# Expert layer of a two-block network: 28 of 32 experts in 64-row blocks, both parts of the rows as 128 stationary columns, experts ordered by count, some low parts on GpSimd

## The chip, the cores and the metric

The kernel runs on one core of a Trainium2 chip. The metric is the device time of one execution in microseconds (us); lower is better. The time before is the median of three runs.

## What is computed

The reference is a network of two blocks on 512 tokens of 1024 features, in fp32. The first block has a hybrid mixer and then a mixture of 32 experts, and only this mixture is touched by the change. Each token chooses one of four groups and in it two of eight experts, so there are 1024 pairs of a token and an expert.

```python
def hierarchical_moe(h, w_rg, b_rg, w_re, b_re, w_e_gate, w_e_up, w_e_down):
    ...
    top_p, top_e = lax.top_k(jax.nn.softmax(le_sel, axis=-1), TOP_K)      # TOP_K = 2 of 8 in the group
    w_tok = p_g * top_p / jnp.sum(top_p, axis=-1, keepdims=True)
    ...
    def expert_rows(args):                                               # xb: rows of expert e
        xb, e = args
        return (jax.nn.silu(xb @ w_e_gate[e]) * (xb @ w_e_up[e])) @ w_e_down[e]
    ...
    contrib = ys[dest].astype(jnp.float32) * w_flat[order][:, None]
    return jax.ops.segment_sum(contrib, tok_sorted, num_segments=T).astype(h.dtype)
```

An expert has 1024 x 512 gate weights, as many up weights and 512 x 1024 down weights: 6 MiB in fp32 (6.29 MB), 201 MB for all. On the reference's inputs the router gives the experts, in order of their index, 26, 27, 11, 42, 12, 21, 30, 25, 12, 26, 30, 16, 13, 20, 39, 20, 67, 62, 44, 57, 26, 65, 40, 21, 31, 39, 29, 27, 27, 42, 46 and 31 tokens.

## The kernel before

Every dense product is made from fp32r parts. A chunk of 128 x 1024 weights is copied to a high part `whi` by ScalarE (L105, in `split`) and the rest is taken to a low part `wlo` by VectorE as raw less `whi` (L106). The other operand has two such parts too. A product is then three passes (`three`, L1672): high by high, high by low, low by high; low by low is left out.

The expert stage is `moe_experts` (L1725). It takes the experts by index. The order on the engines is the scheduler's, which follows the order of the program.

- `ex_rows` (L1650) makes the rows of three experts at once (GR = 3): a 0/1 matrix `s` of places (L1647, 128 x 336 per expert) selects the tokens, and for each of eight feature tiles eight matmuls of 252 columns (L1661) gather 84 rows (R = 84) of each of the three experts into PSUM tile `xg`. ScalarE writes the high part (L1665) and VectorE the low part (L1666). The eight steps run beside the experts of the group before, one at each `side` call.
- `ex_up` (L1680) takes four chunks of 1 MiB of gate and up weights, each in two halves, so eight weight tiles of 128 x 1024. For each, `three` issues 3 passes x 2 outputs = 6 matmuls of 512 columns (L1677, tile `gu`) with the 84 rows as stationary columns. At the end come the silu from PSUM (L1695) and the product with the up half (L1696).
- `ex_turn` (L1699) transposes the result to features on partitions (four transposes, L1704) and splits it (128 x 336).
- `ex_down` (L1709) takes two chunks of 1 MiB of down weights, so four weight tiles of six matmuls each (tile `py`), copies both halves of the result out of PSUM (L1721, ScalarE) and scatters the rows to DRAM by an indirect DMA issued from GpSimd (L1722).

So an expert has 12 weight tiles, 72 matmuls of 512 columns and six DMAs of 1 MiB, all issued in order by SyncE (L93). The down products of expert e - 1 follow the up products of expert e. Pool `raw` holds five chunks and pool `w` three pairs of parts, so that the split of a tile waits for the products of the tile three before it. VectorE, ScalarE and GpSimd work in their program order.

An expert with more than 84 tokens gets further blocks in a run-time loop, `moe_more` (L1760), after the stage. The router (`router`, L1536) ahead of the stage makes `qv`, the places by token and expert; `router_rest` (L1587) makes the tokens' weights, the rows' list `lst` for the scatter and the list of further blocks, after expert 1.

Of the kernel before, what the change touches and what calls it, by code (L numbers as in the profile page):

```python
# [9 lines left out]
F32 = mybir.dt.float32  # L10
# [9 lines left out]
T = 512  # L20
NT = 4
# [6 lines left out]
class Net:  # L28
# [32 lines left out]
    def setup(self, raw=5, w=3, res=10):  # L61
# [11 lines left out]
        # row h of a [40, T] tile of high parts, row 32 + h of low parts, summed onto every partition  # L73
# [48 lines left out]
    def dense_steps(self, p, w, x, first=True, last=True, off=0):  # L122
        """p += w^T x ; w = (hi, lo) with 128 columns per k tile, x = list of (hi, lo)."""
# [45 lines left out]
    def colsums(self, p, src, first=True, last=True, c0=0):  # L169
        """p[:, c0 + i] += sum over the partitions of src, tokens of tile i on partitions."""  # L170
# [4 lines left out]
    def sumsq(self, p, hs, gain=None, c0=0, first=True, last=True, direct=False):  # L175
        """Columns c0.. of p: the sum over all features of (h * gain)^2, tokens on partitions."""
# [15 lines left out]
    def bcast_cols(self, r):  # L192
        """[128 tokens, NT] columns -> [128, T] rows on every partition (PSUM)."""
# [68 lines left out]
    def narrow(self, src, n, x):  # L262
        """[128, NT * n] in PSUM: n columns of weights (src: n per k tile) on x."""
# [28 lines left out]
    def conv(self, z, taps, bias=None):  # L292
        """sum_j z[t - (n-1-j)] * taps[j] + bias ; taps: list of [128, 1]."""
# [14 lines left out]
    def ffn(self, hs, gain, w_up, taps, bias, w_down):  # L308
        """hs: 8 tiles [128, T]; w_up(i) / w_down(half, m) -> DRAM chunks. Returns the new residual tiles."""
# [44 lines left out]
# order of the first steps: decays, products, preparation and inversion of the first heads  # L354
# [3 lines left out]
def merge(*gens, fill=None):  # L358
    """Runs generators side by side, each spread evenly over the whole; fill = (generator, steps) ends with them."""
# [15 lines left out]
class Delta:  # L375
    def delta_consts(self):
        """Masks of the block inversion: for each block size the block left of the diagonal, and its transpose."""
# [15 lines left out]
        # same block, and place of the row in its block  # L393
# [8 lines left out]
    def rows(self, name, p, n):  # L402
        """Both parts of n rows in PSUM, for row_bcast."""
# [10 lines left out]
    def delta_first(self, w_gate16, w_head):  # L414
        """Weights of the step sizes and decays, and of q and k of head 0, the latter still in one part."""
# [76 lines left out]
    def dl_decays(self, p, r, dtB, alogB):  # L492
        """Step sizes beta and the decays' sums gc along each chunk, tokens on partitions."""
# [39 lines left out]
    def softplus(self, x, shape):  # L533
        """max(x, 0) + log1p(exp(-|x|)), the logarithm by its series in e / (2 + e)."""
# [57 lines left out]
    def dl_gates(self, w_head, ot, on):  # L592
        """The gates, and the heads' outputs times them."""
# [478 lines left out]
class Mixer:  # L1072
# [292 lines left out]
    def mixer(self, c):  # L1365
# [69 lines left out]
        for f in range(KD):  # L1435
# [8 lines left out]
            x1.append(t)  # L1444
            self.moe_feed(f, t)
        return x1, mod


NE = 32
R = 84  # L1450
GR = 3
BIG = 1024.0
FAR = 4096.0


class Moe:
# [579 lines left out]
```

## Time and profile before

| | us |
|---|---|
| time, median of 3 runs (range) | 2421.01 (2420.18 to 2422.82) |
| span of the profiled execution | 2423.5 |
| PE busy / VectorE / ScalarE / GpSimd | 2309.5 / 1751.2 / 1235.3 / 166.1 |
| expert stage, first to last silu of an expert | 469.2 to 1068.0 |
| moved by DMA | 374.31 MB |

The span of the profiled execution is its own time; it stands 2.5 us above the median of the three runs. Busy time of PE counts matmuls as they are pipelined: a matmul of 512 columns shows as 0.39 us, but one starts every 0.23 us. How long a row of operations takes is thus read from the starts, not from the sum of durations. The stretch from about 450 to 1075 us is the expert stage; the router lies just before it, the combination of the experts' rows just after it.

### The profile page before, as it was taken

The page shows a single profiled execution, that of the slowest core. Times are in us where ns is not written, and L with a number is a line of the kernel's source. Part 1 is how long each engine was busy: PE and PEld are TensorE (multiplying, and loading weights), DVE is VectorE, ACT ScalarE, POOL GpSimd, SP SyncE. Part 2 cuts the span into 40 slices and gives each one's busy share as a digit, 9 for nine tenths or more (in the row PEclk, how much of TensorE's full clock was granted, in tenths as well). Part 3 has the DMA queues.
Part 4 walks back from the last instruction along what each step waited for, and adds up shares of the span by engine and source line. Part 5 has one row for each costly group of instructions (what it writes and reads, how often), then busy time and mean ns, then how long its engine had stood idle before and what let it go on. Part 6 is the DMA issues. An engine that isn't in the chain of part 4 may idle for free.

```text
span 2423.5 us, 30698 instructions
## 1 busy us (share of the span) xinstructions
PE 2309.5 (95%) x11514; PEld 1832.1 (76%) x11514; DVE 1751.2 (72%) x2954; ACT 1235.3 (51%) x1966; POOL 166.1 (7%) x277
## 2 busy tenths in 40 slices
PE   3999999799999999989899999999999999999998
PEld 2788778576766677755788887888888888888886
DVE  7698874788888888876677767773775775763764
ACT  2253433577777777775444433442444664442441
POOL 4000100000000000000423310000000000000000
PEclk9999999899999999999999999999999999999998
DMA  7634142388888889874111111223212112223221
GB/s 283 234 120 141 36 156 106 137 302 321 330 322 329 325 332 338 336 278 175 53 53 36 53 53 70 88 71 129 98 61 94 70 53 105 82 72 134 83 76 43
DMA packets 64071, 374.31 MB, mean 154 GB/s; under 512 B 9648, under 2 KB 10032, under 8 KB 26032
## 3 DMA queue, kind: packets, MB, share of 16 engines
q1 hardware_dynamic: 60048, 367.97, 41.4%
q0 software_dynamic: 3584, 4.20, 0.5%
q8 instruction: 92, 1.51, 0.3%
q14 instruction: 59, 0.48, 0.1%
q10 hardware_dynamic: 288, 0.14, 0.0%
HBM read 365.85 MB, written 13.25 MB: 156 GB/s over the span
## 4 chain that ended last, share of the span: by engine, by line
PE 46%; DVE 4%; POOL 2%; ACT 2%; issue 1%; DMA 0%; SPq 0%; DVEq 0%; POOLq 0%; ACTq 0%
PE mm L135 13%; PE mm L132 13%; PE mm L129 13%; PE wk L1045 1%; PE wk L743 1%; POOL blk_x L712 1%; POOL blk_t L710 1%; PE wk L748 1%; ACT act L1012 0%; PE wk L993 0%; PE wk L1029 0%; PE po L780 0%; POOL act L714 0%; PE wk L752 0%; DVE act L303 0%
## 5 line engine op out<-in xcount | busy, mean ns | idle before, releaser
L105 ACT CAST whi<-raw 128x1024 fp32r<-128x1024 f32 (+2 forms) x653 | 664.9, 1025 | 725.3 <-PE mm L132 524.2
L106 DVE TENSOR_TENSOR wlo<-raw,whi 128x1024 fp32r<-128x1024 f32 (+2 forms) x652 | 768.7, 1190 | 216.9 <-ACT whi L105 205.5
L132 PE MATMUL mm<-act,whi 128*128 128x512 f32 x1968 | 777.6, 395 | 6.4 <-DVE act L106 4.2
L129 PE MATMUL mm<-act,whi 128*128 128x512 f32 x1968 | 778.6, 396 | 2.1 <-DVE res L472 1.2
L135 PE MATMUL mm<-act,wlo 128*128 128x512 f32 x1968 | 776.6, 395 | 0.3 <-DVE wlo L106 0.3
L132 PEld LDWEIGHTS mm<-act,whi 128*128 128x128 f32 x1968 | 371.6, 189 | 84.8 <-DVE act L106 5.7
L129 PEld LDWEIGHTS mm<-act,whi 128*128 128x128 f32 x1968 | 371.5, 189 | 78.2 <-ACT whi L105 2.7
L135 PEld LDWEIGHTS mm<-act,wlo 128*128 128x128 f32 x1968 | 371.4, 189 | 75.9 <-issue 2.6
L1677 PE MATMUL gu<-whi,act 128*84 128x512 f32 x1024 | 296.9, 395 | 0.4 <-DVE act L1666 0.4
L303 DVE SCALAR_TENSOR_TENSOR act<-act,vec,act 128x511 f32<-128x511 f32 (+2 forms) x272 | 205.9, 759 | 19.1 <-ACT act L298 12.5
L1677 PEld LDWEIGHTS gu<-whi,act 128*84 128x84 f32 x1024 | 151.0, 152 | 70.3 <-DVE act L1666 0.9
L1677 PE MATMUL gu<-wlo,act 128*84 128x512 f32 x512 | 160.2, 394 | 0.0
L1677 PE MATMUL py<-whi,act 128*84 128x512 f32 x512 | 144.2, 392 | 1.0 <-ACT act L105 1.0
L340 DVE TENSOR_TENSOR act<-mm,act 128x512 f32<-128x512 f32 x88 | 60.4, 689 | 84.3 <-PE mm L135 83.9
L1677 PEld LDWEIGHTS gu<-wlo,act 128*84 128x84 f32 x512 | 76.4, 151 | 42.9 <-DVE wlo L106 4.4
L1661 PEld LDWEIGHTS xg<-s,act 128*128 128x128 f32 x704 | 95.9, 192 | 13.5 <-issue 3.0
L1677 PEld LDWEIGHTS py<-whi,act 128*84 128x84 f32 x512 | 76.4, 151 | 37.8 <-ACT act L105 1.1
L105 ACT CAST act<-act 128x512 fp32r<-128x512 f32 x68 | 41.5, 620 | 116.3 <-DVE act L349 93.7
L1661 PE MATMUL xg<-s,act 128*128 128x252 f32 (+1 forms) x704 | 97.2, 282 | 2.9 <-DVE s L1647 2.9
L1181 DVE SCALAR_TENSOR_TENSOR act<-act,dw_half,act 128x482 f32<-128x482 f32 (+14 forms) x120 | 89.2, 744 | 0.5
L300 ACT ACTIVATE act<-act,vec 128x512 f32<-128x512 f32 x96 | 78.0, 814 | 12.2 <-DVE act L340 8.4
L1677 PE MATMUL py<-wlo,act 128*84 128x512 f32 x256 | 80.0, 394 | 1.7 <-DVE wlo L106 1.7
(484 smaller groups left out, 2256.4 us busy)
## 6 DMA issues: line engine op xcount, KB each, us to landing
raw<-in_w_gu_dram SPq DMA_DIRECT2D x128, 1024.0 KB, 5.2
raw<-in_w_dn_dram SPq DMA_DIRECT2D x64, 1024.0 KB, 5.4
raw<-in_f_up_dram SPq DMA_DIRECT2D x44, 1024.0 KB, 4.8
raw<-in_f_dn_dram SPq DMA_DIRECT2D x32, 704.0 KB, 4.0
ada<-in_w_ada_dram SPq DMA_DIRECT2D x32, 512.0 KB, 5.6
raw<-in_a_h_dram SPq DMA_DIRECT2D x16, 1024.0 KB, 5.0
raw<-in_w_ada_dram SPq DMA_DIRECT2D x8, 1024.0 KB, 9.0
raw<-in_w_glu_dram SPq DMA_DIRECT2D x4, 1024.0 KB, 7.4
```

Source lines behind the costliest of these rows:

```text
L105: self.nc.scalar.copy(out=hi, in_=src)
L106: self.nc.vector.tensor_tensor(out=lo, in0=src, in1=hi.bitcast(F32), op=ALU.subtract)
L129: mm(out=p, lhsT=wh[:, s], rhs=xh, start=first and k == 0, stop=False)
L132: mm(out=p, lhsT=wh[:, s], rhs=xl, start=False, stop=False)
L135: mm(out=p, lhsT=wl[:, s], rhs=xh, start=False, stop=last and k == n - 1)
L300: nc.scalar.activation(out=y, in_=z, func=ACTF.Identity, scale=taps[n - 1], bias=bias)
L303: nc.vector.scalar_tensor_tensor(out=y[:, s:], in0=z[:, :T - s], scalar=taps[j], in1=y[:, s:], op0=ALU.mult, op1=ALU.add)
L340: nc.vector.tensor_tensor(out=z, in0=p, in1=rb, op=ALU.mult)
L710: nc.gpsimd.tensor_tensor(out=x2[:, :, j + 1:], in0=R[:, :, j, j + 1:], in1=X[:, :, j:j + 1].to_broadcast([128, NT, B - 1 - j]), op=ALU.mult)
L1181: nc.vector.scalar_tensor_tensor(out=y[:, s:], in0=u[:, :T - s], scalar=taps[:, j, i:i + 1], in1=y[:, s:], op0=ALU.mult, op1=ALU.add)
L1661: nc.tensor.matmul(out=p[:, :n * R], lhsT=hT[k // 4][i][e][:, (k % 4) * 128:(k % 4) * 128 + 128], rhs=s[:, i, :n * R], start=i + e == 0, s ...
L1677: self.nc.tensor.matmul(out=o[:R], lhsT=x, rhs=y[:, i * T:(i + 1) * T], start=first and p == 0, stop=last and p == 2)
```

## The change

It replaces the 84-row blocks. Most hunks that only take out comments and docstrings are left out here.

- Experts are put into slots. Slots 0 and 1 are experts 0 and 1; the others follow by falling count (`moe_order`: a permutation from ranks, made with VectorE and small matmuls, while the rows of slots 0 and 1 are made from the unordered `q0`). SyncE reads the index of the expert of a slot from SBUF and addresses the weights by it.
- Slots 0 to 3 have blocks of 128 rows (RB) and the three passes as before. Slots 4 to 31 have blocks of 64 rows (RS). Their high and low parts lie side by side as 128 stationary columns, so there are two passes, with `whi` and with `wlo`, and low by low is no longer left out. The upper 64 partitions of the result belong to the low parts and are added to the lower 64: for gate and up by a product with `fold` (two unit matrices on top of each other) that turns at the same time, for the down product by a copy (ScalarE) and an addition (VectorE).
- Rows are made for groups of two (slots 0 to 3) or four slots, 256 columns a matmul; the steps are spread over the slots of the group before.
- In `ex_split` the low part of every fourth weight tile (2 and 6 of the up products, 2 of the down products) is made by GpSimd instead of VectorE.
- An expert with more rows than its slot has gets further blocks of 128 rows in `moe_more`.

```diff
+RB, RS = 128, 64
+NBIG, NFIX = 4, 2
+GROUPS = [[0, 1], [2, 3]] + [list(range(s, s + 4)) for s in range(NBIG, NE, 4)]
...
+    def moe_order(self, q, kr, **_):
+        nc = self.nc
+        t, t2, kc, rk = self.small([128, NE]), self.small([128, NE]), self.small([128, 1]), self.small([128, 1])
+        nc.vector.tensor_tensor(out=t, in0=kr, in1=self.mod32, op=ALU.mult)
+        nc.vector.tensor_reduce(out=kc, in_=t, axis=AX.X, op=ALU.add)
+        nc.vector.tensor_scalar(out=t2, in0=kr, scalar1=kc, scalar2=None, op0=ALU.is_gt)
+        nc.vector.tensor_reduce(out=rk, in_=t2, axis=AX.X, op=ALU.add)
+        self.perm = self.mconst("perm", [128, 128])
+        nc.vector.tensor_scalar(out=self.perm, in0=self.agree, scalar1=rk, scalar2=None, op0=ALU.is_equal)
...
     def ex_rows(self, hT, qs, xs, r):
...
-            nc.scalar.activation(out=hi, in_=p[:, :n * R], func=ACTF.Identity, bias=b)
+            nc.scalar.activation(out=x4[:, :, 0], in_=p3, func=ACTF.Identity, bias=b)
+            nc.vector.scalar_tensor_tensor(out=x4[:, :, 1], in0=p3, scalar=b, in1=x4[:, :, 0].bitcast(F32), op0=ALU.add,
+                                           op1=ALU.subtract)
...
+    def ex_products(self, outs, l, w, first, last):
+        wh, wl = w
+        n = l.shape[-1]
+        ps = ((l, wh), (l, wl)) if n == 2 * RS else ((l[:, :RB], wh), (l[:, :RB], wl), (l[:, RB:], wh))
+        for p, (x, y) in enumerate(ps):
+            for i, o in enumerate(outs):
+                self.nc.tensor.matmul(out=o, lhsT=x, rhs=y[:, i * T:(i + 1) * T], start=first and p == 0,
+                                      stop=last and p == len(ps) - 1)
+
+    def ex_split(self, src, c):
+        hi, lo = self.fixed[1] if self.fixed else self.w_pair()
+        self.nc.scalar.copy(out=hi, in_=src)
+        e = self.nc.gpsimd if c % 4 == 2 and not self.fixed else self.nc.vector
+        e.tensor_tensor(out=lo, in0=src, in1=hi.bitcast(F32), op=ALU.subtract)
+        return hi, lo
...
+    def ex_act(self, pg, pu, r):
+        nc = self.nc
         s, a = self.act(), self.act()
+        if r == RB:
+            nc.scalar.activation(out=s, in_=pg, func=ACTF.Silu)
+            nc.vector.tensor_tensor(out=a, in0=s, in1=pu, op=ALU.mult)
+            return a, None
+        nc.scalar.copy(out=s, in_=pg)
+        nc.vector.tensor_copy(out=a, in_=pu)
+        return s, a
+
+    def ex_turn(self, a, u):
...
+        for j, t in enumerate((a, u)):
+            for k in range(4):
+                nc.tensor.matmul(out=p[:, j * 256 + k * RS:j * 256 + (k + 1) * RS], lhsT=t[:, k * 128:k * 128 + 128],
+                                 rhs=self.fold, start=True, stop=True)
+        s, h = self.act(), self.act(F32R)
+        g, m = s[:, :256], s[:, 256:]
+        nc.scalar.activation(out=g, in_=p[:, :256], func=ACTF.Silu)
+        nc.vector.tensor_tensor(out=m, in0=g, in1=p[:, 256:], op=ALU.mult)
+        h4 = h.rearrange("p (k e c) -> p k e c", k=4, e=2)
+        self.split(h4[:, :, 0], h4[:, :, 1], m.rearrange("p (k c) -> p k c", k=4))
...
     def ex_down(self, a, w_dn, rows):
...
-            nc.scalar.copy(out=y[:R, i * T:(i + 1) * T], in_=ys[i][:R])
...
+            t = self.tl("y", "y", [128, D])
+            nc.scalar.copy(out=t[:RS], in_=ys[RS:])
+            nc.vector.tensor_tensor(out=y[:RS], in0=ys[:RS], in1=t[:RS], op=ALU.add)
+        nc.gpsimd.indirect_dma_start(out=self.yd, out_offset=bass.IndirectOffsetOnAxis(ap=rows[:r], axis=0), in_=y[:r],
...
+        def expert(e):
+            if e < NFIX:
+                return e
+            if e not in ids:
+                ids[e] = nc.values_load(self.order[0:1, e:e + 1], engines=(mybir.EngineType.SP,), min_val=0, max_val=NE - 1,
+                                        skip_runtime_bounds_check_because="a permutation of the 32 experts, by ranks of distinct keys")
+            return ids[e]
```

## Rows read from the trace of the kernel before

**Rows 1.** The page: busy us, share and instructions of each engine.

```profile
PE 2309.5 (95%) x11514; PEld 1832.1 (76%) x11514; DVE 1751.2 (72%) x2954; ACT 1235.3 (51%) x1966; POOL 166.1 (7%) x277
```

**Rows 2.** Busy time by stretch: span, engines, granted clock, DMA share, GB/s.

```profile
550.00:650.00 100.00, 99.51 (x491) 69.29 (x490) 86.85 (x92) 78.40 (x95) 4.64 (x5) 1.00 0.89 331
1100.00:1110.00 10.00, 9.04 (x36) 3.60 (x35) 6.79 (x10) 7.59 (x14) 1.59 (x2) 1.00 1.01 428
```

**Rows 3.** Waits from 550 to 1030 us: total us, times, longest.

```profile
ACT whi L105 <- PE gu L1677: 73.6, 138, 0.9
```

**Rows 4.** The silu at each expert's end: duration ns, first and last start.

```profile
L1695 ACT ACTIVATE act<-gu x32: 577/584/598, 469.2 to 1068.0; 84x512 f32<-84x512 f32 x32
```

**Rows 5.** Timeline: start, us, engine, line; runs of equal operations merged.

```profile
1034.94 1.07 PE L1677 MATMUL py<-whi,act 128*84 128x512 f32 x4
455.07 1.10 PE L1661 MATMUL xg<-s,act 128*128 128x252 f32 x8
1187.31 1.00 PE L743 MATMUL wk<-act,act 128*128 128x64 f32 x8
787.20 3.48 DVE L106 TENSOR_TENSOR wlo<-raw,whi 128x1024 fp32r<-128x1024 f32 x3
790.40 3.07 ACT L105 CAST whi<-raw 128x1024 fp32r<-128x1024 f32 x3
```

**Rows 6.** Groups from 200 to 1150 us, by shape: busy us, mean ns of one.

```profile
L1677 PE MATMUL gu<-whi,act 128*84 128x512 f32 x1024 | 296.9, 395 | 0.4 <-DVE act L1666 0.4
L135 PE MATMUL mm<-act,wlo 128*128 128x512 f32 x304 | 121.3, 399 | 0.0
L106 DVE TENSOR_TENSOR wlo<-raw,whi 128x1024 fp32r<-128x1024 f32 x422 | 508.8, 1223 | 106.9 <-ACT whi L105 99.5
L1666 DVE SCALAR_TENSOR_TENSOR act<-xg,mod,act 128x252 fp32r<-128x252 f32 x80 | 37.8, 475 | 3.2 <-ACT act L1665 3.2
L1721 ACT COPY y<-py 84x512 f32<-84x512 f32 x64 | 34.2, 585 | 7.5 <-PE py L1677 4.8
L1722 POOL DMA_INDIRECT yd<-y,lst x32 | 30.4, 949 | 565.7 <-ACT y L1721 559.6 <-DVEq L1767 6.1
L1696 DVE TENSOR_TENSOR act<-act,gu 84x512 f32<-84x512 f32 x32 | 21.6, 674 | 0.2 <-ACT act L1695 0.2
L106 DVE TENSOR_TENSOR act<-xg,act 128x336 fp32r<-128x336 f32 x32 | 16.0, 500 | 0.3 <-ACT act L105 0.3
L1647 DVE TENSOR_TENSOR s<-slot,act 128x336 fp32r<-128x336 f32 x32 | 15.0, 502 | 0.0
```

**Rows 7.** Timeline: GpSimd's elementwise work beside VectorE's.

```profile
1098.42 2.06 DVE L1829 SCALAR_TENSOR_TENSOR res<-wk,mod,res 128x512 f32<-128x512 f32 x3
1099.04 1.28 POOL L1818 TENSOR_TENSOR act<-act,act 128x512 f32<-128x512 f32 x1 [12.47 <-ACT act L1817]
...
1232.19 0.62 POOL L699 TENSOR_TENSOR act<-blk_e,place 128x256 f32<-128x256 f32 x1 [6.97 <-DVE blk_e L696]
1232.22 1.14 DVE L303 SCALAR_TENSOR_TENSOR act<-act,vec,act 128x511 f32<-128x511 f32 x1
1278.65 1.28 POOL L714 TENSOR_TENSOR act<-blk_x,blk 128x512 f32<-128x512 f32 x1
1278.73 1.74 DVE L303 SCALAR_TENSOR_TENSOR act<-act,vec,act 128x511 f32<-128x511 f32 x1
1350.89 1.22 DVE L106 TENSOR_TENSOR wlo<-raw,whi 128x1024 fp32r<-128x1024 f32 x1
1351.05 2.17 POOL L714 TENSOR_TENSOR act<-blk_x,blk 128x512 f32<-128x512 f32 x1
```

**Rows 8.** The group of L303 on the page: busy us, mean ns.

```profile
L303 DVE SCALAR_TENSOR_TENSOR act<-act,vec,act 128x511 f32<-128x511 f32 (+2 forms) x272 | 205.9, 759 | 19.1 <-ACT act L298 12.5
```

**Rows 9.** Busy time by stretch around gaps of PE; the columns of rows 2.

```profile
332.00:339.00 7.00, 5.34 (x13) 4.23 (x14) 6.28 (x8) 1.67 (x2) 0.00 (x0) 0.51 0.18 65
...
1350.00:1356.00 6.00, 4.70 (x36) 4.18 (x35) 3.91 (x14) 2.44 (x13) 3.65 (x6) 1.00 0.46 160
```

More of the change, by code (lines that the diff above doesn't have):

```diff
@@ L1463, in moe_prep @@
             nc.gpsimd.iota(c[name], pattern=pattern, base=base, channel_multiplier=ch, allow_small_or_imprecise_dtypes=True)
-        self.rev, self.slot, self.tokv = c["rev"], c["slot"], c["tokv"]
+        self.rev, self.slot, self.tokv, self.bonus, self.step = (c[n] for n in ("rev", "slot", "tokv", "bonus", "step"))
+        for e in range(NFIX):
+            nc.vector.tensor_scalar(out=self.bonus[:, e:e + 1], in0=self.bonus[:, e:e + 1], scalar1=float(FIRST * (NFIX - e)),
+                                    scalar2=None, op0=ALU.add)
@@ L1660, in ex_rows @@
                 for e in range(2):
[L1661 to L1662 removed]
+                    nc.tensor.matmul(out=p[:, :n * r], lhsT=hT[k // 4][i][e][:, (k % 4) * 128:(k % 4) * 128 + 128],
+                                     rhs=s[:, i, :n * r], start=i + e == 0, stop=i + e == NT)
             x = self.act(F32R)
[L1664 removed]
@@ L1709, in ex_down @@
     def ex_down(self, a, w_dn, rows):
         nc = self.nc
-        ah, al = a
-        ys = [self.tl("ps", "py", [128, T], F32, bufs=2) for _ in range(2)]
+        r = RS if not isinstance(a[0], tuple) else RB
+        ys = self.tl("ps", "py", [128, D], F32, bufs=1)
+        outs = [ys[:, i * T:(i + 1) * T] for i in range(2)]
         for q in range(2):
@@ L1725, in moe_experts @@
-    def moe_experts(self, hT, w_gu, w_dn, rest):
-        group = lambda e: [self.qv[:, i, 0:4] for i in range(e, min(e + GR, NE))]
-        x, xn = None, [[] for _ in range(GR)]
-        first = self.ex_rows(hT, group(0), xn)
+                wp = self.ex_split(w[:, j * 1024:(j + 1) * 1024], k)
+                if r == RS:
+                    self.ex_products(outs, a[k], wp, k == 0, k == 3)
+                else:
+                    self.three(outs, a[k], wp, k == 0, k == 3)
+        y = self.tl("y", "y", [128, D])
@@ new lines, in ex_down, with three @@
+        if r == RB:
+            nc.scalar.copy(out=y, in_=ys)
+        else:
+            t = self.tl("y", "y", [128, D])
+            nc.scalar.copy(out=t[:RS], in_=ys[RS:])
+            nc.vector.tensor_tensor(out=y[:RS], in0=ys[:RS], in1=t[:RS], op=ALU.add)
+        nc.gpsimd.indirect_dma_start(out=self.yd, out_offset=bass.IndirectOffsetOnAxis(ap=rows[:r], axis=0), in_=y[:r],
+                                     in_offset=None, bounds_check=2 * T - 1, oob_is_err=False)
+    def three(self, outs, l, w, first, last):
+        (lh, ll), (wh, wl) = l, w
+        for p, (x, y) in enumerate(((lh, wh), (lh, wl), (ll, wh))):
+            for i, o in enumerate(outs):
+                self.nc.tensor.matmul(out=o, lhsT=x, rhs=y[:, i * T:(i + 1) * T], start=first and p == 0,
+                                      stop=last and p == 2)
@@ L1730, in moe_experts, with weights @@
+    def moe_experts(self, hT, w_gu, w_dn, order, rest):
+        nc = self.nc
+        xn = [[] for _ in GROUPS[0]]
+        first = self.ex_rows(hT, [self.q0[:, :, e] for e in GROUPS[0]], xn, RB)
         next(first)
+        order()
+        ids, rows = {}, None
         a = t = None
-        def side(q):
-            nonlocal t
-            if e:
-                next(rows, None)
+        def expert(e):
[5 more added lines that the diff above has]
+            return ids[e]
+        def weights(w, e, m):
+            i = expert(e)
+            return w[i, m] if e < NFIX else w[bass.ds(i, 1), m].rearrange("a p c -> (a p) c")
+        def side(q):
+            nonlocal t, due
+            if e and rows:
+                due += 8 / sides
+                while due > 0.5:
+                    next(rows, None)
+                    due -= 1
@@ L1743, in before @@
                 next(first, None)
+        starts = {g[0]: i for i, g in enumerate(GROUPS)}
+        due = 0
         for e in range(NE + 1):
-            if e % GR == 0:
-                x, xn = xn, [[] for _ in range(GR)]
-                if e + GR < NE:
-                    rows = self.ex_rows(hT, group(e + GR), xn)
+            if e in starts:
+                for _ in rows or ():
+                    pass
+                i = starts[e]
+                x, xn = xn, []
+                rows = None
+                if i + 1 < len(GROUPS):
+                    g = GROUPS[i + 1]
+                    xn = [[] for _ in g]
+                    rows = self.ex_rows(hT, [self.qv[:, s, 0:4] for s in g], xn, 256 // len(g))
+                sides, due = 4 * (len(GROUPS[i]) - (e == 0)), 0
             if e < NE:
-                b = self.ex_up(x[e % GR], lambda m: w_gu[e, m], side, before)
+                b = self.ex_up(x[e - GROUPS[i][0]], lambda m: weights(w_gu, e, m), side, before)
                 if e == 1:
```

196 lines of the change are left out of this document (120 added, 76 removed).

## The prediction, made before the change was run

> **What bounds the kernel now.** The page first: PE is busy for 95% of the span, VectorE for 72%, ScalarE for 51%, GpSimd for 7% [rows 1]. Such shares are means over stages, so the second view is the stretch that the change touches. From 550 to 650 us PE has 99.5 of 100 us, VectorE 87, ScalarE 78, GpSimd 5, and the DMA engines are at 0.89 with 331 GB/s [rows 2]. Third, who waits: ScalarE's split of weights waits for PE's products, 138 times in 480 us [rows 3]. So in the expert stage PE is the bound, and VectorE and the transfers are not far behind. Last, its pace: from the first silu to the last there are 31 experts in 598.8 us, 19.3 us each [rows 4].
>
> PE's own work explains that pace. Four matmuls of 512 columns show 1.07 us, of which the last 0.39 is its own length, so one starts every 0.23 us; eight gathers of 252 columns start every 0.117 us [rows 5]. 72 x 0.23 = 16.6 us, and 88 gather steps x 8 x 0.117 over 32 experts = 2.6 us; with the four transposes 19.4. There is nothing in the 19.3 us but PE.
>
> **What the change takes from PE.** An expert with 64 rows has two passes, 48 x 0.23 = 11.0 us. The gathers of four experts are 8 steps x 8 matmuls of 256 columns, 64 x 0.118 / 4 = 1.9 us. The turn is eight fp32 products of 64 columns; eight such show 1.00 us, one every 0.11 us [rows 5], so 0.9. PE needs 13.8 us instead of 19.4. 128 stationary columns instead of 84 cost nothing that the rows show: a matmul of 512 columns lasts 399 ns with 128 and 395 ns with 84 [rows 6].
>
> Were PE the only limit, 28 experts would save 28 x 5.5 = 154 us. So the question is what is late next.
>
> **The transfers.** An expert's 6.29 MB stay. Just after the stage the DMA engines moved 428 GB/s over 10 us [rows 2], at which 6.29 MB take 14.7 us. That is a floor below the next one. SyncE reads an index per slot before it issues; it has one issue every 3.2 us (19.3 / 6), and I put this at nothing, up to 1 us an expert if the read is slow.
>
> **ScalarE.** Three copies of 128 x 1024 show 3.07 us, one every 1.0 us [rows 5]: 12.1 us, and about 2.7 us for gathers, the copies out of PSUM, silu and split (by columns from the 0.585 us of a 512-column copy [rows 6]). 14.8 us: not the next bound either.
>
> **VectorE.** Three low parts show 3.48 us, so one starts every 1.13 us although it lasts 1.22 [rows 5, 6]; I take 0.09 off each operation for that. Nine low parts stay here: 10.2. Low parts of the rows: two of 0.39, in 24 of 28 experts, 0.7. Places: 256 columns by the 336 of now, 0.3. Copy of the up half from PSUM, by the 0.674 of the product that it replaces: 0.6. Product and split of the turn on 256 columns: 0.3 each. Addition of the two halves of the result on 1024 columns, as long as a low part: 1.1. Together 13.5 us [rows 6]. With all 12 low parts it would be 16.9.
>
> **GpSimd.** An elementwise operation with two inputs took 1.28 us for 512 columns and 0.62 for 256 [rows 7]; in a line 1024 take 2.6 us, three 7.8 us, and the scatter 0.95 [rows 6]. It has 18 us for that. But these operations are not free for VectorE. The low part takes `raw` and `whi`, both in SBUF, and rows 7 show what happens when such an operation meets GpSimd: L303, 0.76 us as a rule [rows 8], took 1.74 when it began 0.08 us after a 1.28 us operation of GpSimd, and 1.14 after one of 0.62. The other way round, GpSimd's L714 took 2.17 us when it came during a low part, and ended 1.1 us after it. They run one after the other. VectorE loses 0.38 us to 256 columns and 0.98 to 512; in a line that is 2.2 for 1024 (upper end 2.6, the whole operation). I take 2.25: 6.7 us an expert.
>
> The Trainium skill has this as a rule (SBUF — State Buffer, section Who interferes with whom): an operation of VectorE with two SBUF inputs and one of GpSimd that reads SBUF exclude each other, and the later one waits for the whole instruction. The trace agrees on the exclusion but shows 0.98 of 1.28 us lost. By the page's rule three whole operations of 2.6 us, an estimate, would be 1.1 us more an expert, and the change about 31 us later than by my sum.
>
> VectorE and GpSimd together then have 13.5 + 6.7 = 20.2 us, more than now, unless VectorE does something else while GpSimd works. It can: the three L1829 from 1098.42 on, which take one input from PSUM, took 2.06 us together, less than three times L303's 0.76, though L1818 ran for 1.28 us beside them [rows 7]. Of the 13.5 us such operations are: low parts of the rows 0.7, copy 0.6, product 0.3, addition 1.1, in all 2.7. How many fall beside GpSimd is the uncertain term, between 0 and 2.7.
>
> I lay the operations out by hand, with the ring of three pairs. A split waits for the low part of the tile three before it, so VectorE is one or two tiles ahead of PE. What needs PE's end of tile 3, 7 or the last down tile becomes ready when VectorE has done two tiles more, just where GpSimd's tile (2, 6, 2 of the down) comes next. The addition lands beside up tile 2, the first rows' low part beside up tile 6, the copy beside down tile 2: 1.1 + 0.4 + 0.6 = 2.1 us. The product, the second rows' low part and the split come while low parts are queued. That gives 20.2 - 2.1 = 18.1, and I allow 0.4 (0 to 0.8) for VectorE waiting for others: 18.5 us an expert.
>
> GpSimd's queue: the scatter of an expert stands behind the addition, and a low part that stands behind the scatter would wait for both. By hand the addition ends before GpSimd's tile 2 does, so I put nothing here; the other order makes the addition uncovered.
>
> **Sum.** The last 28 experts: from the fourth silu on the pace now is 19.3 (the mean of [rows 4]); 28 x (18.5 - 19.3) = -22. The first four keep three passes: PE 16.6 us plus gathers; they have 16 gather steps where the stage now has 12, +4, and VectorE with GpSimd at about 20 us is as late as PE, +4 (0 to 8). `moe_order` adds some ten operations of 0.2 to 0.3 us on VectorE while the first gathers run, +1 (0 to 3); the evacuation after the last expert, copy then addition instead of two copies, +1. Constants at the start, +1. In all -22 + 11 = -11: the profiled execution would go from 2423.5 to 2412, and the median, 2.5 us below its span now, to 2410.
>
> **The rivals.** (a) Slower: the uncovered sum. If the scheduler puts the addition and the copy behind a low part, 0.4 us at most lies beside GpSimd: 20.2 - 0.4 + 0.4 = 20.2, 28 x 0.9 + 11 = +36, 2457. It decides where less than 1.7 us of the 2.7 is covered (28 x 0.4 us = the 11 us of the rest). For it: VectorE keeps a fixed order, and the program order has these operations behind low parts. Against: my layout. 0.33.
>
> (b) The exclusion costs little, because VectorE anyway waits at those times, and the stage falls to what ScalarE and the transfers allow, 15.5 us: -106 + 11, 2326. Against: all of rows 7 show exclusion. 0.10.
>
> (c) Near break-even, 18.8 to 19.1 us: 2418 to 2426, 0.15.
>
> (d) PE, which now waits, gets the low clock. The granted clock fell to 0.51 of 2.4 GHz, that is 1.2 GHz, in 7 us where PE had gaps of about 2 us, and stayed at 1.00 with PE busy for 78% of 6 us [rows 9]. A wait for GpSimd's tile is some 1.3 us (its 2.6 us less the products of one or two tiles, 0.9 us each, that PE still has). If it fell, 13.8 us would be up to 27.6 and the stage over 100 us longer. 0.03.
>
> (e) It doesn't do what it says: further blocks. In order of count, slots 2 and 3 get the experts with 67 and 65 tokens, and the next has 62, under 64. So no pass of `moe_more`, unless the chip counts otherwise; a pass would cost at least the 14.7 us of its transfers. 0.01.
>
> **How the numbers follow.** The forecast, 18.1 to 18.8 us an expert (2398 to 2418), has 0.38. A difference of 0.2%, 5 us, is about what a measurement of this kernel can tell from no change. Faster: 0.38 + 0.10 = 0.48. Same: 0.15. Slower: 0.33 + 0.03 + 0.01 = 0.37. As both signs are likely, the forecast's own range is 2398 to 2418. The wide one leaves out (b) below and the worst of (a), (d) and (e) above: all 2.7 us covered, no waits and none of the additions, 28 x (17.5 - 19.3) = -50, gives 2371; nothing covered with 0.2 us of waits, 20.4, gives 2463, and the upper price of the exclusion a little more: 2367 to 2468.
>
> **What would show it.** Two passes: 32 matmuls of `gu` and 16 of `py` for each of slots 4 to 31, and PE no longer busy all the time in the stage. The exclusion: low parts on VectorE of up to 3.5 us, and GpSimd's of 2.6 us or more, one beginning where the other ends. The layout: the addition, the copy and a rows' low part beside GpSimd's operations. A pace between silus of neighbours near 18.5 us. I am wrong if VectorE and GpSimd run side by side at their own speed, if PE is still busy all the time, or if VectorE is idle for more than 1 us an expert.

## The result, and the profile after

The changed kernel takes 2537.09 us (median of 4 runs) where the kernel before takes 2420.60: a ratio of 1.048, 95% interval 1.046 to 1.049. It is slower, and above the range of the prediction. The profiled execution has a span of 2535.3 us, 111.8 more than before.

The page's engine row of the changed kernel answers [rows 1]: PE has 12 us less, VectorE 63 us more although 96 low parts have left it, GpSimd 262 more.

```profile
PE 2297.5 (91%) x11062; PEld 1840.3 (73%) x11062; DVE 1814.4 (72%) x2919; ACT 1225.9 (48%) x1949; POOL 428.6 (17%) x379
```

Busy time by stretch, the view of [rows 2], for 100 us in the middle of the stage:

```profile
850.00:950.00 100.00, 82.50 (x359) 60.75 (x358) 80.89 (x70) 64.72 (x80) 38.56 (x18) 0.90 0.79 284
```

PE is no longer the bound, and neither is any other engine: VectorE has 81 of 100 us, ScalarE 65, the transfers 284 GB/s instead of 331. When nothing is full, the time is in waits. The granted clock is 0.90, too.

The pace, the view of [rows 4]: the silu of the first four experts (L1795), and the copy of the gate half out of PSUM that ends the up products of the other 28 (L1798); duration in ns, first and last start:

```profile
L1795 ACT ACTIVATE act<-gu x4: 589/590/600, 472.2 to 541.5; 128x512 f32<-128x512 f32 x4
...
L1798 ACT COPY act<-gu x28: 576/587/589, 562.1 to 1171.9; 128x512 f32<-128x512 f32 x28
```

From the fourth silu to the last copy, 28 experts take 1171.9 - 541.5 = 630.4 us, **22.51 us each** instead of 19.27: +91. The first four take 69.3 instead of 59.1 (+10), they begin 3 us later, and from the last copy to the last scatter it is 20.4 instead of 13.9 us (+7): together 111 of the 112.

The low parts, the view of [rows 6] (562 to 1050 us; duration is the number after the comma), and below them the same line over the whole run with its shortest, median and longest duration in ns:

```profile
L1774 DVE TENSOR_TENSOR wlo<-raw,whi 128x1024 fp32r<-128x1024 f32 x194 | 323.7, 1692 | 52.7 <-ACT whi L1772 52.6
L1774 POOL TENSOR_TENSOR wlo<-raw,whi 128x1024 fp32r<-128x1024 f32 x65 | 166.1, 2555 | 192.3 <-PE py L1766 94.7 <-ACT whi L1772 86.1 <-PE gu L1766 7.8
```

```profile
L1774 DVE TENSOR_TENSOR wlo<-raw,whi x288: 1204/1216/3762, 416.6 to 1184.4; 128x1024 fp32r<-128x1024 f32 x144
...
L1774 POOL TENSOR_TENSOR wlo<-raw,whi x96: 2352/2372/3887, 431.3 to 1184.4; 128x1024 fp32r<-128x1024 f32 x96
```

Most of VectorE's low parts (205 of 288) take 1.2 us as before, the others up to 3.76. One expert's timeline shows how (start, us; in brackets the idle time and what ended it; weight loads and some lines left out):

```profile
853.47 0.69 DVE L1799 COPY act<-gu 128x512 f32<-128x512 f32 x1 [0.82 <-PE gu L1766]
...
857.36 2.37 POOL L1774 TENSOR_TENSOR wlo<-raw,whi 128x1024 fp32r<-128x1024 f32 x1 [5.79 <-PE py L1766]
...
858.21 2.60 DVE L1774 TENSOR_TENSOR wlo<-raw,whi 128x1024 fp32r<-128x1024 f32 x1 [1.07 <-ACT whi L1772]
...
859.78 0.73 PE L1766 MATMUL py<-wlo,act 128*128 128x512 f32 x2 [1.43 <-POOL wlo L1774]
...
862.89 1.22 DVE L1844 TENSOR_TENSOR y<-py,y 64x1024 f32<-64x1024 f32 x1 [0.60 <-ACT y L1843]
...
864.38 1.63 POOL L1845 DMA_INDIRECT yd<-y,lst  x1 [4.65 <-ACT act L1751]
865.16 0.47 DVE L1752 SCALAR_TENSOR_TENSOR act<-xg,mod,act 128x256 fp32r<-128x256 f32 x1
...
866.04 2.36 POOL L1774 TENSOR_TENSOR wlo<-raw,whi 128x1024 fp32r<-128x1024 f32 x1
866.22 5.54 DVE L1774 TENSOR_TENSOR wlo<-raw,whi 128x1024 fp32r<-128x1024 f32 x3 [0.59 <-ACT whi L1772]
...
868.45 0.74 PE L1766 MATMUL gu<-wlo,act 128*128 128x512 f32 x2 [1.97 <-POOL wlo L1774]
```

VectorE's low part from 858.21 ends at 860.81, 1.08 us after GpSimd's ended (859.73): it ran behind it. Three from 866.22 take 5.54 instead of 3.48. And the copy (853.47), the addition (862.89) and the rows' low part (865.16), which the prediction had put beside GpSimd's low parts, stand where GpSimd has none: it waits for PE, for the addition, or issues the scatter. (The bracket of the scatter names L1751, which ended last before it, at 864.31; by the program the scatter reads what the addition writes, and that ended at 864.11.)

The low parts are not the only work that is held up. The places (L1730) have two SBUF inputs too, which the prediction did not price; the same line in the changed kernel and in e1, the kernel without GpSimd's low parts, 562 to 1050 us:

```profile
L1730 DVE TENSOR_TENSOR s<-slot,act 128x256 fp32r<-128x256 f32 x16 | 17.2, 1092 | 3.8 <-PE xg L1745 3.8
```

```profile
L1730 DVE TENSOR_TENSOR s<-slot,act 128x256 fp32r<-128x256 f32 x16 | 6.1, 419 | 0.2
```

To compare kernels, VectorE's time per expert is taken apart, from the starts and durations of all its instructions between the fourth and the last end of an expert's up products: busy; lost (of the busy time, what low parts take over 1.215 us each; the places come on top, 0.46 us an expert in the changed kernel); idle. Beside it the pace and the time:

| kernel | GpSimd's tiles | pace | busy | lost | idle | time |
|---|---|---|---|---|---|---|
| before | none | 19.27 | 16.60 | 0.10 | 2.67 | 2421 |
| after | up 2, 6, down 2 | 22.51 | 18.49 | 4.35 | 4.02 | 2537 |
| e1 | none | 18.65 | 17.04 | 0.01 | 1.61 | 2419 |
| e2 | as after, 8 columns read | 19.16 | 13.83 | 0.04 | 5.33 | 2435 |
| e5 | as after, 4 pairs | 23.70 | 19.36 | 5.28 | 4.34 | 2571 |
| e6 | as after, PE kept busy | 22.37 | 18.86 | 5.03 | 3.51 | 2535 |
| e8 | up 6 | 20.17 | 17.88 | 1.90 | 2.29 | 2464 |
| e11 | up 0, 4, down 0 | 19.79 | 15.96 | 1.87 | 3.83 | 2462 |
| e12 | up 0, down 0 | 18.79 | 15.46 | 0.44 | 3.33 | 2432 |
| e9 | none, copy on ScalarE | 17.89 | 16.34 | 0 | 1.55 | 2401 |
| e13 | as e12, copy on ScalarE | 18.99 | 15.94 | 1.52 | 3.05 | 2439 |

### The profile page after: what moved, and what is told of

It is laid out like the page before. It is cut to its first block, busy times and chain, and to the rows that moved or that the text cites. A ratio compares the mean times of both kernels' runs of the same rounds, so it can differ in the third digit from the quotient of the medians.

```text
span 2535.3 us, 30370 instructions
## 1 busy us (share of the span) xinstructions
PE 2297.5 (91%) x11062; PEld 1840.3 (73%) x11062; DVE 1814.4 (72%) x2919; ACT 1225.9 (48%) x1949; POOL 428.6 (17%) x379
## 4 chain that ended last, share of the span: by engine, by line
PE 44%; DVE 4%; POOL 2%; ACT 2%; issue 1%; DMA 0%; SPq 0%; DVEq 0%; POOLq 0%; ACTq 0%
PE mm L135 12%; PE mm L132 12%; PE mm L129 12%; PE wk L1045 1%; POOL blk_x L712 1%; POOL blk_t L710 1%; PE wk L743 1%; PE wk L748 1%; ACT act L1012 0%; POOL act L714 0%; PE wk L993 0%; DVE act L303 0%; PE wk L1029 0%; PE po L780 0%; PE wk L1995 0%
## 5 line engine op out<-in xcount | busy, mean ns | idle before, releaser
L105 ACT CAST whi<-raw 128x1024 fp32r<-128x1024 f32 (+2 forms) x269 | 264.2, 985 | 589.9 <-PE mm L132 525.6
L1774 DVE TENSOR_TENSOR wlo<-raw,whi 128x1024 fp32r<-128x1024 f32 x288 | 472.1, 1662 | 84.9 <-ACT whi L1772 84.6
L1772 ACT CAST whi<-raw 128x1024 fp32r<-128x1024 f32 x384 | 391.7, 1047 | 119.5 <-PE gu L1766 59.8
L106 DVE TENSOR_TENSOR wlo<-raw,whi 128x1024 fp32r<-128x1024 f32 (+2 forms) x268 | 306.0, 1143 | 129.4 <-ACT whi L105 125.1
L1774 POOL TENSOR_TENSOR wlo<-raw,whi 128x1024 fp32r<-128x1024 f32 x96 | 242.3, 2524 | 464.7 <-ACT whi L1772 301.4
L1766 PE MATMUL gu<-wlo,act 128*128 128x512 f32 x512 | 200.8, 478 | 81.7 <-POOL wlo L1774 58.3
L303 DVE SCALAR_TENSOR_TENSOR act<-act,vec,act 128x511 f32<-128x511 f32 (+2 forms) x272 | 205.1, 756 | 19.1 <-ACT act L298 12.5
L1766 PEld LDWEIGHTS gu<-wlo,act 128*128 128x128 f32 x512 | 100.1, 221 | 147.1 <-POOL wlo L1774 80.8
L1766 PE MATMUL gu<-whi,act 128*128 128x512 f32 x576 | 202.8, 441 | 2.6 <-ACT whi L1772 2.6
L1766 PEld LDWEIGHTS gu<-whi,act 128*128 128x128 f32 x576 | 120.1, 216 | 37.5 <-ACT whi L1772 11.1
L1745 PE MATMUL xg<-s,act 128*128 128x256 f32 x576 | 89.7, 287 | 2.6 <-DVE s L1730 1.9
```

The source lines that it names most:

```text
L105: self.nc.scalar.copy(out=hi, in_=src)
L106: self.nc.vector.tensor_tensor(out=lo, in0=src, in1=hi.bitcast(F32), op=ALU.subtract)
L303: nc.vector.scalar_tensor_tensor(out=y[:, s:], in0=z[:, :T - s], scalar=taps[j], in1=y[:, s:], op0=ALU.mult, op1=ALU.add)
L1745: nc.tensor.matmul(out=p[:, :n * r], lhsT=hT[k // 4][i][e][:, (k % 4) * 128:(k % 4) * 128 + 128], rhs=s[:, i, :n * r], start=i + e == 0, s ...
L1766: self.nc.tensor.matmul(out=o, lhsT=x, rhs=y[:, i * T:(i + 1) * T], start=first and p == 0, stop=last and p == len(ps) - 1)
L1772: self.nc.scalar.copy(out=hi, in_=src)
```

## Experiments

### Is it GpSimd, and is it what it reads?

**No GpSimd.** All low parts on VectorE:

```diff
-        e = self.nc.gpsimd if c % 4 == 2 and not self.fixed else self.nc.vector
+        e = self.nc.vector
```

> The changed kernel with all low parts of the weights on VectorE. Theory E (exclusion: VectorE's low parts and GpSimd's run one after the other, and PE waits for both): VectorE has 12 low parts, 16.9 us an expert by the prediction's sum, PE 14.9 (the turn counts 16 instructions, not 8); pace of the small experts 17 to 18 us, time 2375 to 2400 us, the granted clock at 1.00 nearly throughout the stage. Theory L (the two-pass layout is slow by itself: the longer way from the up products over copies, fold, silu and split to the down products, and from the down products over copy and addition to the scatter): pace stays above 20 us, time above 2450 us.

Measured: 2419.31 us, ratio 0.999 (0.998 to 1.000). The whole loss goes, and the low parts are back at their own length:

```profile
L1774 DVE TENSOR_TENSOR wlo<-raw,whi x384: 1202/1217/1227, 416.6 to 1069.3; 128x1024 fp32r<-128x1024 f32 x192
```

So 118 us of the result belong to three low parts an expert on another engine. But the rest of the change only breaks even: 18.65 us an expert, not the 17 to 18 expected. VectorE has 17.04 and stands for 1.61.

**GpSimd as long, but hardly reading.** Its operation reads 8 columns, and four memsets bring it to the same length; the other columns of these low parts are left out of the products:

```diff
-        e = self.nc.gpsimd if c % 4 == 2 and not self.fixed else self.nc.vector
-        e.tensor_tensor(out=lo, in0=src, in1=hi.bitcast(F32), op=ALU.subtract)
+        e, n = (self.nc.gpsimd, 8) if c % 4 == 2 and not self.fixed else (self.nc.vector, 1024)
+        e.tensor_tensor(out=lo[:, :n], in0=src[:, :n], in1=hi[:, :n].bitcast(F32), op=ALU.subtract); [e.memset(lo[:, 8 + i * 508:516 + i * 508].bitcast(F32), 0.0) for i in (0, 1, 0, 1) if n == 8]
```

> The changed kernel, where GpSimd takes the same tiles, waits for the same parts and works as long (about 2.3 us) but reads only 8 columns of them and fills the other 1016 with zeros by four fills of 508 columns, so that these low parts are left out of the output. Theory E: GpSimd's reading is what stops VectorE, so VectorE's low parts last 1.22 us again (now 1.67 in the mean), pace 18 to 20 us, time 2390 to 2450. Theory Q (GpSimd's order and length: PE waits for a low part that takes 2.4 us and stands in a queue behind the scatter; exclusion adds little): pace stays at 21.5 to 22.5 us, time 2510 to 2540.

Measured: 2434.56 us, ratio 1.005 (1.003 to 1.007), as theory E had it. GpSimd is in the same tiles for as long (7.8 us an expert against 7.5), and VectorE no longer notices it:

```profile
L1774 DVE TENSOR_TENSOR wlo<-raw,whi x288: 1203/1219/1254, 416.6 to 1083.3; 128x1024 fp32r<-128x1024 f32 x144
```

So of the 118 us some 103 come with what GpSimd reads, and 15 are left when it hardly reads, although VectorE then has three low parts less to do: with only 13.8 us of work it stands for 5.3, and the pace is still 19.2.

**The same in the kernel before.** Only `ex_split` is taken over into it; blocks and products stay:

```diff
-                wp = self.split_w(w[:, j * 1024:(j + 1) * 1024], 1024)
+                wp = self.ex_split(w[:, j * 1024:(j + 1) * 1024], k)
```

> The kernel before with only one part of the change: the low parts of weight tiles 2 and 6 of the up and 2 of the down products by GpSimd. Theory E: VectorE's own work falls to 12.6 us an expert, GpSimd's exclusion adds 6.7, together 19.3, what PE needs too; pace 19.5 to 21.5 us, time 2430 to 2490. Theory L: GpSimd does no harm where the layout is the old one, time 2415 to 2425.

Measured: 2476.50 us, ratio 1.023 (1.021 to 1.025), 20.98 us an expert, 2.5 of VectorE's time lost. The exclusion does not need the new layout.

**Order and groups alone.** All 32 experts in 128-row blocks with three passes, ordered, no low parts on GpSimd (the hunks of the row limits and of `ex_split`, as in e1, are left out here):

```diff
-NBIG, NFIX = 4, 2
-GROUPS = [[0, 1], [2, 3]] + [list(range(s, s + 4)) for s in range(NBIG, NE, 4)]
+NBIG, NFIX = 32, 2
+GROUPS = [[s, s + 1] for s in range(0, NE, 2)]
...
```

> The changed kernel without the two-pass layout and without GpSimd's low parts: all 32 experts in blocks of 128 rows, three passes, rows made for two experts at a time, experts ordered by count. Both theories: PE is the bound with 72 x 0.23 + 4 x 8 x 0.118 + 0.4 = 20.7 us an expert, 1.4 more than before, so time about 2465 (2455 to 2480). It tells what the order, the constants and the new index reads cost: what it lies above 2421 + 32 x 1.4 = 2466 is theirs.

Measured: 2477.04 us, ratio 1.023 (1.021 to 1.025), at the expected size. The 11 us above 2466 would by the expectation be the cost of order, constants and index reads; no run takes them apart. PE is busy for 100 of 100 us, 20.8 an expert. 64-row blocks without GpSimd save 58 us against this, and the 84-row blocks of before were already 56 under it.

### The idle time: ring, clock, number

**Four pairs of weight parts.** A raw chunk becomes the fourth pair (so four of five raw chunks are left), in the changed kernel (e5) and in the one without GpSimd (e7; its hunk of `ex_split` is that of e1):

```diff
-        return self.tl("w", "whi", [128, 1024], F32R), self.tl("w", "wlo", [128, 1024], F32R)
+        self.nw = (getattr(self, 'nw', 0) + 1) % 4; s = getattr(self, 'spare', None) if self.nw == 0 else None; return (s[:, :1024], s[:, 1024:]) if s is not None else (self.tl("w", "whi", [128, 1024], F32R), self.tl("w", "wlo", [128, 1024], F32R))
...
-        ids, rows = {}, None
+        ids, rows, self.spare = {}, None, self.tl("raw", "raw", [128, 2048], F32R)
...
```

> The changed kernel whole, with four pairs of weight parts in the expert stage instead of three; the fourth is one of the five raw chunks, of which four are left. Of the 22.5 us an expert, VectorE is busy for 18.5 (9 low parts and the rest 14.1, 4.45 us of it lost while GpSimd holds it up) and idle for 4.0. Theory R (the idle time comes from the ring: a split waits for the products of the tile three before it, and these for GpSimd's late low part): a fourth pair takes most of it away, pace 19.5 to 20.8 us an expert, 2450 to 2490 us. Theory K (the idle time comes from the low clock of PE, 3.8 us an expert, and PE goes on waiting at each of GpSimd's tiles): 22.0 to 22.8 us an expert, 2520 to 2545 us.

> The changed kernel with all low parts on VectorE and four pairs of weight parts instead of three (four raw chunks left). With three pairs it takes 18.65 us an expert, with PE and VectorE busy for 17.0 each and 2419 us. Theory R (the 1.65 us in which VectorE is idle come from the ring of three pairs): 17.1 to 17.7 us an expert, 2378 to 2396 us, faster than both kernels. Theory S (they come from the serial places, turn and evacuations, which no deeper ring hides): 18.3 to 18.8 us, 2410 to 2424 us.

Measured: e5 2570.99 us, 34 slower than with three pairs, which neither theory had; e7 2425.58 (ratio 1.001, 1.0005 to 1.002), its pace 18.66 against 18.65. A deeper ring, paid with a raw chunk, takes nothing off the pace in either kernel. What VectorE waits for between 562 and 1150 us, first in the changed kernel, then in e5 (to 1200 us):

```profile
DVE wlo L1774 <- ACT whi L1772: 66.0, 71, 2.0
DVE act L1799 <- PE gu L1766: 23.1, 25, 1.5
DVE y L1844 <- ACT y L1843: 11.9, 20, 0.7
```

```profile
DVE act L1799 <- PE gu L1766: 52.9, 25, 3.1
DVE raw L1774 <- ACT raw L1772: 42.9, 49, 1.5
DVE y L1844 <- ACT y L1843: 14.3, 22, 1.0
```

With a deeper ring VectorE runs further ahead, and then stands longer at the copy (L1799), for PE to end the up products. The wait has moved, and more low parts meet (lost 5.28 instead of 4.35).

**PE kept busy.** Four products of a zero tile between the two passes of each of GpSimd's tiles (the hunks that make the zero tile and set `late` are left out):

```diff
...
+        ps = (ps[0], (self.zero, wh), (self.zero, wh), ps[1]) if self.late and n == 2 * RS else ps
```

> The changed kernel, with four matmuls of a zero stationary tile (128 rows by 512 columns, added to the sums as zero) between the high and the low pass of each of GpSimd's three tiles, so that PE is not idle while it waits for that low part; they are 12 x 0.23 = 2.8 us an expert of extra work on PE. Theory K (the low clock makes the products late, half of 3.8 us an expert): the granted clock stays at 1.00, pace 20.6 to 21.5 us, 2485 to 2512 us. Theory R (the clock is only a sign of the waits, which come from exclusion and ring): clock 1.00, but pace 22.0 to 23.0 us, 2520 to 2555 us.

Measured: 2535.10 us. Rows of both kernels by stretch: the changed one before and in a stretch of low clock, then this one:

```profile
853.30:869.80 16.50, 12.40 (x64) 9.04 (x63) 14.08 (x13) 11.79 (x16) 6.36 (x3) 1.00 0.76 268
869.80:873.20 3.40, 3.40 (x9) 2.67 (x9) 2.64 (x3) 2.04 (x3) 2.33 (x1) 0.50 0.77 248
```

```profile
750.00:850.00 100.00, 87.30 (x398) 61.95 (x397) 86.16 (x71) 66.14 (x80) 43.23 (x19) 1.00 0.79 279
```

In the changed kernel the clock is granted at 1.2 GHz for 106 of the stage's 630 us, in stretches of 3.4 or 6.8 us, this one behind the wait at 868.45. With the extra products 14 us of it remain, and the time is the same. The added products are not what holds the pace either: at 70 of GpSimd's 84 tiles of the stage PE still waits behind them for GpSimd's part, as after up tile 2 here:

```profile
938.67 1.09 PE L1766 MATMUL gu<-whi,zero 128*128 128x512 f32 x4
...
940.82 0.73 PE L1766 MATMUL gu<-wlo,act 128*128 128x512 f32 x2 [1.05 <-POOL wlo L1774]
```

VectorE's idle time falls by 0.5 us an expert, and its lost time rises by 0.7. So a clock that is full for nearly all of the stage does not win the loss back.

**One tile instead of three** (only up tile 6):

```diff
-        e = self.nc.gpsimd if c % 4 == 2 and not self.fixed else self.nc.vector
+        e = self.nc.gpsimd if c == 6 and not self.fixed else self.nc.vector
```

> The changed kernel with one low part of an expert on GpSimd (tile 6 of the up products, that the rows' low part was to cover) instead of three. Theory E (each of GpSimd's tiles costs its exclusion and a wait of the ring, alike): a third of the way from 18.65 to 22.5, 19.6 to 20.3 us an expert, 2443 to 2470 us. Theory C (this tile is covered as the prediction had it, and the loss comes from the others or from their number): 18.0 to 18.8 us, 2400 to 2424 us.

Measured: 2464.27 us, ratio 1.017 (1.015 to 1.019), 20.17 us an expert. One tile takes 1.13 us from VectorE, and costs 1.90 of exclusion and 0.7 of idle time. Both engines run long when they meet:

```profile
L1774 DVE TENSOR_TENSOR wlo<-raw,whi x352: 1204/1218/3402, 416.6 to 1112.8; 128x1024 fp32r<-128x1024 f32 x176
...
L1774 POOL TENSOR_TENSOR wlo<-raw,whi x32: 2370/3348/3369, 463.9 to 1097.1; 128x1024 fp32r<-128x1024 f32 x32
```

### The place of GpSimd's tiles

**Tiles 0, 4 and 0:**

```diff
-        e = self.nc.gpsimd if c % 4 == 2 and not self.fixed else self.nc.vector
+        e = self.nc.gpsimd if c % 4 == 0 and not self.fixed else self.nc.vector
```

> The changed kernel with GpSimd's low parts at other tiles: 0 and 4 of the up products and 0 of the down products instead of 2, 6 and 2. Theory E (each of GpSimd's tiles costs its exclusion and a wait of the chain, wherever it lies; the work that the prediction put beside it does not fall there in either kernel): 22.0 to 23.2 us an expert, 2520 to 2555 us. Theory L (the place decides, by what of VectorE's work without two SBUF inputs falls beside GpSimd): away from 22.5 by over 1 us, under 2507 or over 2565 us.

Measured: 2461.75 us, ratio 1.017 (1.014 to 1.020): 75 us less with as many low parts on GpSimd. Theory E falls; the place decides. GpSimd's down tile 0 now runs beside the copy and VectorE's waits around it:

```profile
879.21 3.12 POOL L1774 TENSOR_TENSOR wlo<-raw,whi 128x1024 fp32r<-128x1024 f32 x1 [2.48 <-ACT whi L1772]
...
880.92 0.69 DVE L1799 COPY act<-gu 128x512 f32<-128x512 f32 x1 [0.83 <-PE gu L1766]
...
882.25 1.23 DVE L1774 TENSOR_TENSOR wlo<-raw,whi 128x1024 fp32r<-128x1024 f32 x1 [0.64 <-ACT whi L1772]
```

By starts and ends, GpSimd's low parts in the changed kernel (7.5 us an expert) lie for 5.3 us beside low parts of VectorE, 0.4 beside its other work and 1.8 beside an idle VectorE; here (8.1 us) it is 3.3, 1.7 and 3.3. Of the 0.4 all but 0.1 is beside the places, which are held up as low parts are; of the 1.7, 1.3 is beside work with an input in PSUM (copy, product, rows' low part), which keeps its length.

**The two well placed ones alone** (e12), and the same with the copy of the up half out of PSUM on ScalarE (e13):

```diff
-        e = self.nc.gpsimd if c % 4 == 2 and not self.fixed else self.nc.vector
+        e = self.nc.gpsimd if c == 0 and not self.fixed else self.nc.vector
...
-        nc.vector.tensor_copy(out=a, in_=pu)         # e13 alone
+        nc.scalar.copy(out=a, in_=pu)
```

> The changed kernel with two low parts of an expert on GpSimd, tile 0 of the up products and tile 0 of the down products, where in the kernel with 0, 4 and 0 they lie beside VectorE's copy out of PSUM, its product and its waits; tile 4, which meets low parts, is back on VectorE. Theory C (place decides: a GpSimd tile that lies beside other work costs little and takes 1.1 us from VectorE): 17.4 to 18.6 us an expert, 2385 to 2419 us. Theory D (each GpSimd tile costs, by its length and the exclusion, more than it takes off, though less at a good place): 18.9 to 19.5 us an expert, 2425 to 2445 us.

> The same two low parts on GpSimd, and the copy of the up half out of PSUM on ScalarE. Without GpSimd this copy on ScalarE gives 17.9 us an expert and 2401 us. Theory C: VectorE has 2.2 us less to do, 16.6 to 17.6 us an expert, 2368 to 2396 us. Theory D: 18.0 to 19.0 us, 2403 to 2431 us.

Measured: e12 2432.24 us (ratio 1.004, 1.002 to 1.005), e13 2438.89 (1.007, 1.005 to 1.008), against 2419 and 2401 without GpSimd: theory D, with e12's pace of 18.79 just below its range and e13 8 us above it. Little is lost in e12 (0.44, and 0.2 in the places), VectorE has 1.6 us less to do, and the pace does not fall. In e13 the copy is no longer there to lie beside GpSimd's tile: 2.5 us of GpSimd's time instead of 1.4 meet low parts, and 1.52 are lost. Where the time went, by what VectorE waits for, from 562 us to 1050 in e1 and to 1070 in e12:

```profile
DVE act L1799 <- PE gu L1766: 19.3, 24, 0.8
DVE wlo L1774 <- ACT whi L1772: 13.6, 28, 1.0
DVE y L1844 <- ACT y L1843: 8.4, 19, 1.0
```

```profile
DVE y L1844 <- ACT y L1843: 47.8, 21, 2.4
DVE act L1799 <- PE gu L1766: 20.7, 25, 1.0
DVE wlo L1774 <- ACT whi L1772: 17.4, 27, 1.2
```

It stands at the addition, for the copy that ScalarE makes when PE has ended the down products: 1.8 us an expert instead of 0.3.

### A faster version

In the kernel without GpSimd VectorE's longest wait is that at the copy L1799. e9 moves this copy to ScalarE, as e13 does; e10 also puts off the addition (`flush` runs the addition and the scatter of the expert before; its other hunks are left out):

```diff
...
         def before(q):
+            if q == 1: self.flush()
...
```

> The changed kernel with all low parts on VectorE, and the copy of the up half out of PSUM on ScalarE instead of VectorE. Without that move it takes 18.65 us an expert: VectorE 17.0 busy and about 1.6 idle, of it 0.8 standing at this copy until PE has ended the up products. Theory V (VectorE's fixed order is the bound): the copy's 0.69 and most of that wait go, 17.0 to 17.7 us an expert, 2374 to 2395 us, faster than both kernels; ScalarE rises from 14.5 to 15.1. Theory S (the chain of products, turn and splits is the bound, and VectorE waits in it): 18.3 to 18.8 us, 2409 to 2424 us.

> As the kernel with the copy on ScalarE and all low parts on VectorE, and the addition of the result's halves comes one weight tile later in VectorE's order, so that it does not stand waiting for ScalarE's copy of the upper half (0.3 to 0.4 us an expert). Theory V: 16.7 to 17.4 us an expert, 2365 to 2387 us, up to 10 us less than without the later addition. Theory S: 18.3 to 18.8 us, 2409 to 2424 us.

Measured: e9 2401.13 us, ratio 0.993 (0.991 to 0.994), e10 2399.67, ratio 0.991 (0.990 to 0.993): faster than both kernels, by less than expected. The order on VectorE is the same in both (the addition already stood that late once the copy was gone), so e10 is a second measurement of e9. The pace is 17.89, neither theory's: the copy's 0.7 us went, VectorE's idle time did not (1.55). It waits elsewhere now, 562 to 1030 us:

```profile
DVE wlo L1774 <- ACT whi L1772: 37.8, 31, 1.5
```

ScalarE's next splits are queued behind the two copies, which wait for PE. Why VectorE's idle time stays near 1.6 us is left open.

## Why the prediction was wrong

**Right.** PE is no longer the bound, the transfers and ScalarE (14.65 us an expert; 14.8 said) are not either. VectorE's own work with all 12 low parts is 17.04 (16.9 said). The first four experts cost 10 us (8 said), the start 3 (2 said). No further block came: there are 32 scatters. VectorE and GpSimd exclude each other where both read SBUF, and a tile's price holds: e8 shows 1.90 us on VectorE and 0.70 (3.07 us mean against 2.37) on GpSimd, where 2.25, at most 2.6, was taken. Coverage was rightly named as a term that decides; e11 shows it.

The place where the Trainium skill was weighed (SBUF — State Buffer, section Who interferes with whom) goes to the page: the later instruction waits for the whole of the other one. Behind 84 of GpSimd's 96 low parts in the changed kernel a low part of VectorE ends, and each of them ends 1.08 or 1.09 us after GpSimd's, nearly its own whole length; the 2.60 us from 858.21 is one, the 3.76 us another (by its record it even starts 0.3 us before GpSimd's). Rows 7 showed it already: L303 from 1278.73 ends 0.54 us after GpSimd's L714, and its usual length is 0.75. What was too long in the estimate by the page's rule was the 2.6 us: GpSimd's low part takes 2.37 alone. So the price of 2.25 was near the truth, though it was drawn from a loss in proportion.

**The failing steps, by size.** First, the waits. "I allow 0.4 (0 to 0.8) for VectorE waiting for others" is 4.02 in the changed kernel; more than 1 us was one of the prediction's own signs of being wrong. VectorE's busy time came out near the sum, 18.5 against 18.1; with a wait of 0.4 the pace would have been 18.9, just above the forecast's 18.1 to 18.8. 1.6 of the 4.0 is there without GpSimd (e1), the rest comes with it: PE waits for GpSimd's tile, ScalarE's next split for PE, VectorE for the split (66.0 us against 13.6 in e1 in the rows above). That the wait lies in this chain is read from the rows; that neither a deeper ring (with a raw chunk less) nor a full clock takes it off the time is shown (e5, e6); why it has this size is open.

Second, the layout by hand. Of the 2.7 us of work that could lie beside GpSimd's low parts, not 2.1 but 0.1 did; the places, which the prediction had not among the work that is held up, took 0.76 us an expert where e1 has 0.30. The step that failed is the assumption that an operation and a GpSimd tile that become ready at about the same time run at the same time. GpSimd is in order too: the scatter stands before up tile 2 and waits for the addition, so the two that were to overlap come one after the other (862.89, 864.38, 866.04). The price for that queue was put at nothing; the row shows GpSimd's tile beginning when the scatter's 1.63 us end, and PE waiting 1.97 us for it. ScalarE's split of this tile ended at 865.24, so the scatter held GpSimd up by 0.8 us; behind 29 of the 32 scatters GpSimd's next low part begins within 0.02 us. What this queue costs the whole is not shown: no run with GpSimd's low parts moves the scatter. That the sum of busy time came out all the same is luck: 1.8 us of GpSimd's work fell beside an idle VectorE instead.

Third, two small terms: the turn shows as 16 matmuls for its eight products and not 8, 2.0 us instead of 0.9, where PE was not the bound; and the end of the stage is 7 us later, not 1.

```profile
853.88 2.00 PE L1814 MATMUL xg<-fold,act 128*128 128x64 f32 x16
```

**The rivals.** (a), the uncovered sum, had the coverage nearly right (0.4 at most, 0.1 measured) and the waits wrong as the forecast had: 20.2 us instead of 22.5. (b) and (c) fell with the forecast's waits. (d): the clock did fall, at waits of 1.4 to 2.0 us, though the prediction gave it 0.03; its cost was not the 100 us it named: in e6, where all but 14 of the 106 us at 1.2 GHz are gone, the time is the same.

## What to carry to other kernels

Work moved from VectorE to GpSimd brought nothing in any of the numbers and places tried here, where both read SBUF: what it took off came back as lost time and as waits, and its place against VectorE's copies and waits was worth more than its number. A sum of busy times is a floor and not a pace: when a change takes a full engine off the path, the next pace is the sum of the engine that comes next and its waits at each point where, working in order, it needs another engine's end. These waits should be counted one by one. Moving the instruction at which a full engine stands, to one with room, gained 16 to 18 us (e9 against e1); the change without GpSimd's low parts only broke even.

## What the runs showed of the hardware

GpSimd's writes did not hold VectorE up: beside memsets of 524 ns four times a tile the low part stayed at 1219 ns (median) and 1254 at most, beside reads of the same length it went to 3762.

The scatter's issue on GpSimd, 0.95 us before [rows 6], depends on the kernel, by its own line in the changed kernel, in e9 and in e4 (128 rows):

```profile
L1845 POOL DMA_INDIRECT yd<-y,lst x32: 898/1634/1719, 501.7 to 1192.3; - x32
```

```profile
L1845 POOL DMA_INDIRECT yd<-y,lst x32: 896/3102/8444, 497.6 to 1053.5; - x32
```

```profile
L1846 POOL DMA_INDIRECT yd<-y,lst x32: 962/962/1151, 499.3 to 1131.0; - x32
```

The median was 0.93 to 0.96 us in the three kernels that scatter 84 or 128 rows an expert (before, e3, e4), and 1.63 to 3.11 in all that scatter 64 rows, which VectorE writes. It does not go by VectorE's idle time (1.63 in the changed kernel with 4.0 us idle, 1.97 in e12 with 3.3 and in e1 with 1.6). No run here tells the cause apart.
